# A hybrid decoder block on one core: the last four chunks of w_out split during attention and loaded into h's places by pairs of k, output blocks handed out with 17 steps left

## The chip, the cores and the metric

The kernel runs on one core of one Trainium2 chip. The metric is the device time of one execution in microseconds (us); for the kernel before it is the median of three runs. Engines are named as in the profile: PE does matrix products, PEld loads their weights, DVE is the vector engine, ACT the scalar engine, POOL the general one, and SP issues the DMAs.

## What is computed

One decoder block over 1024 tokens of width 1024, in float32: a token mixer, then a squared-ReLU MLP, each with a norm before and after, a modulation from a conditioning vector and a gate.

```python
mod = cond @ w_ada + b_ada                     # six vectors: sh_a, sc_a, gt_a, sh_m, sc_m, gt_m
h = rms_norm(x, g_attn_pre) * (1 + sc_a) + sh_a
proj = h @ w_in                                # qa, ka, va, qb, kb, vb; rotary on part of q and k
oa = banded_attention(qa, ka, va, 127, sink=sink_a)    # mixer A: 8 query heads on 2 kv heads
ob = dilated_mixture_attention(qb, kb, vb)             # mixer B: 8 heads, three dilated windows
mixed = concat([rms_norm(oa, g_mix_a), rms_norm(ob, g_mix_b)])
y = mixed @ w_out
x = x + gt_a * rms_norm(y, g_attn_post)
h = rms_norm(x, g_mlp_pre) * (1 + sc_m) + sh_m
x = x + gt_m * rms_norm(square(relu(h @ w_up)) @ w_down, g_mlp_post)
```

## The kernel before

**Numbers in two parts.** For accuracy every operand of a large product is split into a part that the fast matmul format holds and the rest: a = hi + lo. Each product is three matmuls (hi hi, hi lo, lo hi) of 128 rows by 512 columns. One engine makes hi (a cast, mostly on ACT) and another lo (a subtraction, on DVE or POOL). The weights w_in, w_out, w_up and w_down and the activations all go through this.

**Stages.** At first the modulation and the norm of x are worked out and h, transposed and modulated, is written to the buffer `hw` by `mod_chunk` (L677). `hw` has 8 places of two parts (hi and lo) of 128 partitions by 1024 numbers. Before the change place t holds the 128 tokens of block t for all 8 chunks of k (128 each), so a matmul over 512 tokens (`proj_mm`, L858) reads four places with a stride.

Then come the projections in 6 units u (two of mixer A, one for each kv head, then four of mixer B, two heads each), each of two halves x of the tokens and three tiles c (q, k, v); `proj_tile` (L917) issues the 8 steps over k of one tile, three matmuls a step. `st.d` counts units done (0 to 6). Attention runs beside them: `items` lists pieces of attention (unit, query block, head), 48 in all, each a chain: scores `s_ps` on PE (L1127, L1182), maximum and masking on DVE (`mn`, L1146, L1197), exponentials on ACT (L1153, L1202), scaling on POOL (`p_sb`, L1158, L1214), a transposition on PE (`pt_ps`, L1232, L1239), the split of the result into `ph` by ACT (L1246) and DVE (L1250), and the product with v on PE (`o_ps`, L1262, L1274). ACT and DVE take it out of PSUM to `ot` and a DMA stores it to the scratch tensor `o_dram` (L1301, L1319). `st.att` counts finished items.

The weights of the modulation are loaded in the background too, into the stage slots, and summed up by POOL (`ada_acc`, L1015). A stage slot is one of five buffers of 128 by 1024 numbers (`r_stg`); the rope products of each unit (DVE L762 to L765, then ACT L768 and POOL L771) take them as well.

**The output stage.** `load_wo` (L1339) becomes due when at most two projection tiles are left to hand out. For each of 8 chunks k it loads 128 rows of w_out raw into a stage slot (L1348), and makes hi on ACT (L1353) and lo on DVE (L1356) or on POOL (L1361, L1362), whichever the planner takes, into place k of `hw`. A place of h can only be overwritten when the last projection tile of its half has read it: `r_wo` counts the places that are free, four given by the last step of each of the two tiles of unit 5, c = 2 (L931). `open_out` (L1367) comes when all are split and the projections are done: it closes the pools of the projections, loads the gate (`gate_a`, L1377) and lets `feed_out` (L1399) hand out the 8 output blocks, one of 128 tokens after another, when their items are finished and at most 10 dense steps are left in PE's queue. `out_block` (L1417) loads `o_sb` from `o_dram` (L1423), casts it to `oh` (L1436) and `ol`, takes the sum of squares by a matmul (`pm_o`, L1452), issues 16 steps of y (L1478 to L1480, three matmuls a step), and works out the post-norm, the gate, the residual, the norm before the MLP (`xn`, L1532) and its transposition (`px`, L1541), which gives the MLP's input. Then the MLP's products (`mlp_ps`, L1912 to L1914) fill PE.

**The order.** At build time a planner (`Sched`) plays the work on five engines with cost formulas. An operation is ready by its dependencies (`deps`) and by counted resources (`takes` and `gives`). Each engine takes the ready step with the earliest start, then the lower `prio`; a step that has two engines to choose from goes to the one that ends it first. PE has streams (`dense` for projections, y and the MLP, `s` and `t` for attention, `misc`, `xt`), with a preference among them that depends on how far the projections are ahead of attention (`prefer`, L2064). Functions in `sc.launch` are called again and again until they hand out their work. What comes out is a fixed order for each engine: on the chip every engine, and the DMA queue of SP too, goes through its list in order and waits at each instruction for the semaphores it needs. So one moved operation changes the order of many.

Of the kernel before, what the change touches and what calls it, by code (L numbers as in the profile page):

```python
# [10 lines left out]
F32 = mybir.dt.float32  # L11
F32R = mybir.dt.float32r
# [3 lines left out]
ALU = mybir.AluOpType  # L16
# [3 lines left out]
P = 128  # L20
D = 1024
S = 1024
KC = D // P
TB = S // P
# [150 lines left out]
class Sched:  # L175
# [20 lines left out]
    def op(self, eng, dur, emit, deps=(), **kw):  # L196

        o = self.step(dur, emit, deps, **kw)
        o.alts = None
        if isinstance(eng, str):  # L200
            self.queue[eng].append(o)
        else:
            o.alts = dict(zip(eng, zip(dur, emit)))
            for e in eng:
                self.queue[e].append(o)
        return o.ev
# [113 lines left out]
def t_sb(n):  # L320
    return 0.098 + 0.00083 * n
# [6 lines left out]
def t_dv(n):  # L328
    return 0.066 + 0.00104 * n
# [6 lines left out]
def t_ptt(n):  # L336
    return 0.19 + 0.0021 * n


def t_pts(n):  # L340
    return 0.28 + 0.00083 * n
# [7 lines left out]
def hybrid_block(ctx: ExitStack, tc: tile.TileContext, x, positions, w_ada, b_ada, g_attn_post, w_in, w_out,  # L349
# [94 lines left out]
    def stage(name):  # L444
        if st.stgp is None:
            return ring_r(name)
        return st.stgp.tile([P, 1024], F32, name=name, tag="stg")

    def load(emit, nbytes, deps=(), takes=(), prio=5, gives=(), after=None, n=1):
        return op("SP", nbytes / (345e3 if prio > -500 else 370e3), emit, deps, takes=takes, prio=prio, gives=gives, after=after, n=n)  # L450
# [226 lines left out]
    def mod_chunk(k, eg, half):  # L677
        t0, t1 = (0, TB) if half is None else (4 * half, 4 * half + 4)
        n = (t1 - t0) * P
        ks = slice(k * P, (k + 1) * P)  # L680
        h, hh = xnT[:, k, t0 * P:t1 * P].rearrange("p (b t) -> p b t", t=P), hw[:, t0:t1, 0, ks]
        deps = [eg] + (e_xn[0] + e_xn[1] if half is None else e_xn[half])

        def full(eng):
            if eng is A:
                return lambda: A.activation(h, h, AF.Identity, bias=s_a[:, k:k + 1], scale=g_a[:, k:k + 1])
            return lambda: V.tensor_scalar(h, h, g_a[:, k:k + 1], s_a[:, k:k + 1], ALU.mult, ALU.add)

        eh = op("ACT", t_sb(n) + 2 * AP_COST, lambda: A.activation(hh, h, AF.Identity, bias=s_a[:, k:k + 1],
                                                                  scale=g_a[:, k:k + 1]), deps, prio=0)  # L690
        e = op("ACT", t_sb(n) + 2 * AP_COST, full(A), [eh], prio=0)
        e = op("DVE", t_dv(n), lambda: V.tensor_tensor(hw[:, t0:t1, 1, ks], h, hh.bitcast(F32), ALU.subtract), [e],
               prio=0)
        for x in (0, 1) if half is None else (half,):
            e_hh[k, x], e_hl[k, x] = eh, e
# [162 lines left out]

    def proj_mm(ps, u, c, k, x, part):
        i, n = w_at(u, c, k)  # L860
        t, w = slice(k * P, (k + 1) * P), w_hl[u, i]
        n = slice(n * P, n * P + P)
        h = [hw[:, 4 * x:4 * x + 4, i, t] for i in range(2)]
        ps = ps[:].rearrange("p (b t) -> p b t", t=P)
        if part != 1:
            T.matmul(ps, w[:, 0, n], h[0], start=(k == 0), stop=False)  # L866
            T.matmul(ps, w[:, 1, n], h[0], start=False, stop=False)  # L867
        if part != 0:
            T.matmul(ps, w[:, 0, n], h[1], start=False, stop=(k == KC - 1))  # L869
# [50 lines left out]
    def proj_tile(u, x, c):  # L920
        b = []
        for k in range(KC):
            def emit(k=k):
                if k == 0:
                    b.append(pj.tile([P, 512], F32, name="pj", tag="pj"))
                proj_mm(b[0], u, c, k, x, None)
            gives = []
            if x and k % 4 == 3:
                gives.append((r_w, 1))
            if u == 5 and c == 2 and k == KC - 1:  # L930
                gives.append((r_wo, 4))  # L931
            d = dense(0.681, emit, [w_e[u, w_at(u, c, k)[0]]], takes=[(r_pj, 1)] if k == 0 else [], gives=gives, after=tick)
        evac(u, x, c, lambda: b[0], d, r_pj)

# [401 lines left out]
    NSTG2 = 4  # L1336
    ph2 = Tok()

    def load_wo():  # L1339

        if len(todo_dense) > 2 or ada.i < NADA:
            return False
        ph2.e_wo, ph2.raw = {}, {}
        eh = None
        for k in range(KC):
            def f_l(k=k):
                ph2.raw[k] = stage("wo_st")
                nc.sync.dma_start(ph2.raw[k][:], w_out[k * P:(k + 1) * P])  # L1348
            e = load(f_l, 524288, takes=[(r_stg, 1), (r_wo, 1)], prio=-8)
            g = cols[:, 56 + k:57 + k]  # L1350

            def f_h(k=k, g=g):
                A.mul(hw[:, k, 0], ph2.raw[k][:], g)  # L1353

            def f_lo(k=k, g=g):
                V.scalar_tensor_tensor(hw[:, k, 1], ph2.raw[k][:], g, hw[:, k, 0].bitcast(F32), ALU.mult,  # L1356
                                       ALU.subtract)
            eh = op("ACT", t_sb(D) + AP_COST, f_h, [e] + ([eh] if eh else []), prio=4)

            def f_lo2(k=k, g=g):  # L1360
                G.tensor_scalar(ph2.raw[k][:], ph2.raw[k][:], g, 1.0, ALU.mult, ALU.mult)  # L1361
                G.tensor_tensor(hw[:, k, 1], ph2.raw[k][:], hw[:, k, 0].bitcast(F32), ALU.subtract)  # L1362
            ph2.e_wo[k] = op(("DVE", "POOL"), (t_dv(D) + AP_DV, t_pts(D) + t_ptt(D)), (f_lo, f_lo2), [eh],
                             gives=[(r_stg, 1)], prio=4)
        return True

    def open_out():  # L1367
# [30 lines left out]

    def feed_out():  # L1399
        tb = ph2.tb  # L1400
        if tb < TB and st.att >= 42 + 2 * (tb // 2) and len(sc.pe.get("dense", [])) <= 10:
            out_block(tb)
            ph2.tb += 1
        return ph2.tb == TB
# [308 lines left out]
    def sums(h, p):  # L1713

        t = half(h)
        fr = t.free
        up_ = h % 2 == 0
        own_a = h == 0 or not up_
        if p == "P1":
            fr.update({"T1": joins(r_raw, 2), "T3": joins(r_raw, 1), "B22": joins(r_raw, 3), "T4": joins(r_raw, 1),  # L1720
                       "T2": joins(r_raw, 2)})
            if h == 0:
                t.a = {q: h2[q] for q in h2}
                t.e_a = dict(e_h2)
                t.ring = r_h2
                t.new = ring_r
            elif not up_:
                u = half(h - 1)
                t.a, t.e_a, t.ring = dict(u.c), {}, r_u
                t.new = lambda n: ring_l(n, F32)  # L1730
            if h == 0 or not up_:
                fr.update({"S1": joins(t.ring, 2), "S3": joins(t.ring, 1), "S2": joins(t.ring if h else r_u, 2),
                           "S4": joins(t.ring, 1), "A22": joins(t.ring, 2)})
        if own_a and h:
            for q, e in half(h - 1).e_c.items():
                t.e_a.setdefault(q, e)
        ea, eb = events(h)
        sum_ = partial(add_up, 10 + ml.seq.index((h, p)))
        if p == ("P6" if h else "P5"):
            sum_(t.b, t.e_b, eb, r_raw, None, "T1", "12", "11", ALU.subtract, [], t.sp["B", "11"], "11")  # L1740
            if not h:
                first_sums(t)
        if p == "P6":
            sum_(t.b, t.e_b, eb, r_raw, ring_r, "T2", "22", "T1", ALU.subtract, [fr["B22"], fr["T1"]], None, None)
            if h == 0:
                second_sums(t)
            elif own_a:
                sum_(t.a, t.e_a, ea, t.ring, t.new, "S1", "21", "22", ALU.add, [fr["A22"]], None, None)
                sum_(t.a, t.e_a, ea, t.ring, None, "S3", "11", "21", ALU.subtract, [], [[e] for e in t.e_a["S1"]], "21")
                sum_(t.a, t.e_a, ea, t.ring, None, "S2", "S1", "11", ALU.subtract, [fr["S1"]],  # L1750
                     [x + [t.e_a["S3"][j]] for j, x in enumerate(t.sp["A", "11"])], "11")
        if p == "P7":
            sum_(t.b, t.e_b, eb, r_raw, None, "T3", "22", "12", ALU.subtract, [fr["B22"]], [[e] for e in t.e_b["T1"]],
                 "12")
        if p == "P3" and own_a:
            sum_(t.a, t.e_a, ea, t.ring, None, "S4", "12", "S2", ALU.subtract, [fr["S2"]], t.sp["A", "12"], "12")
        if p == "P4":
            sum_(t.b, t.e_b, eb, r_raw, None, "T4", "21", "T2", ALU.subtract, [fr["T2"]], t.sp["B", "21"], "21")
# [331 lines left out]
```

## Time and profile before

| what | value |
| --- | --- |
| median of three runs | 1146.05 us (1145.21 to 1146.7) |
| the profiled execution | 1144.1 us |
| its span, from the first to the last instruction of the profile | 1142.2 us |
| mean granted TensorE clock | 0.991 of full speed |
| PE busy, share of the span | 97% |
| DMA traffic | 185.29 MB, mean 162 GB/s |
| projections and attention | to about 380 us; attention without projections to about 437 us |
| output stage, then MLP | to about 535 us, then to the end |

The profiled execution is 1.95 us below the median and holds 1.9 us outside its span. A row of a timeline gives start and length in us, engine, line, operation, what it writes and reads, and how many like it follow each other; brackets hold the idle time of the engine before it and what ended it. Matmuls are pipelined: the distance of their starts is what one costs, not its length. L is a line of the kernel before; in the changed kernel the lines behind L1336 stand some 30 lower.

### The profile page before, as it was taken

How to read it: one execution, taken by the hardware profiler on the slowest of the kernel's cores; microseconds unless marked ns; L12 is line 12 of the kernel's file. 1: busy time of each engine (PE TensorE's matmuls, PEld its weight loads, DVE VectorE, ACT ScalarE, POOL GpSimd, SP SyncE). 2: the span in 40 equal slices, each digit the busy share in tenths (PEclk: the TensorE clock that was granted, in tenths of full speed). 3: DMA queues.
4: the chain of work that ended last, by engine and by line, in shares of the span. 5: the costliest groups of instructions: out<-in, count | busy, mean ns of one | idle time of the engine just before them, and what ended most of it. 6: DMA issues, size and time to landing. Idle time of an engine off the chain costs nothing.

```text
span 1142.2 us, 15600 instructions
## 1 busy us (share of the span) xinstructions
PE 1113.5 (97%) x5417; PEld 925.2 (81%) x5417; DVE 819.3 (72%) x1378; ACT 636.1 (56%) x1101; POOL 267.8 (23%) x349
## 2 busy tenths in 40 slices
PE   8999999999999899998999999999999999999996
PEld 7788878888888687887888888888888888888885
DVE  7878666666667766668879664599644896537998
ACT  8868865464556755676675434553244733246542
POOL 2458867565743521112000000000000000000002
PEclk9999999999999899999999999999999999999998
DMA  9565545343423305555780168712469112584103
GB/s 351 187 208 164 164 155 168 136 155 125 141 77 133 127 26 186 185 202 217 284 310 19 56 230 292 280 41 70 152 245 331 55 56 86 202 304 164 37 19 148
DMA packets 90910, 185.29 MB, mean 162 GB/s; under 512 B 8400, under 2 KB 31056, under 8 KB 90832
## 3 DMA queue, kind: packets, MB, share of 16 engines
q1 hardware_dynamic: 90832, 184.30, 46.1%
q8 instruction: 43, 0.70, 0.2%
q14 instruction: 35, 0.29, 0.1%
HBM read 137.08 MB, written 28.31 MB: 145 GB/s over the span
## 4 chain that ended last, share of the span: by engine, by line
PE 77%; DVE 8%; ACT 4%; issue 4%; POOL 3%; DMA 3%; SPq 0%; DVEq 0%; POOLq 0%; ACTq 0%
PE mlp_ps L1913 17%; PE mlp_ps L1914 17%; PE mlp_ps L1912 17%; PE pj L866 4%; PE pj L869 4%; PE pj L867 4%; PE s_ps L1127 3%; PE o_ps L1262 2%; PE y_ps L1478 1%; PE pt_ps L1232 1%; PE y_ps L1479 1%; PE y_ps L1480 1%; PE pt_ps L1235 1%; DMA o_sb<-o_dram 1%; PE o_ps L1267 1%
## 5 line engine op out<-in xcount | busy, mean ns | idle before, releaser
L1912 PE MATMUL mlp_ps<-hw 128*128 128x512 f32 x896 | 349.8, 390 | 0.0
L1913 PE MATMUL mlp_ps<-hw 128*128 128x512 f32 x896 | 348.8, 389 | 0.0
L1914 PE MATMUL mlp_ps<-hw 128*128 128x512 f32 x896 | 348.8, 389 | 0.0
L1912 PEld LDWEIGHTS mlp_ps<-hw 128*128 128x128 f32 x896 | 168.5, 188 | 35.5 <-issue 0.5
L1913 PEld LDWEIGHTS mlp_ps<-hw 128*128 128x128 f32 x896 | 168.4, 188 | 35.2 <-issue 0.5
L1914 PEld LDWEIGHTS mlp_ps<-hw 128*128 128x128 f32 x896 | 168.4, 188 | 34.9
L1676 DVE TENSOR_TENSOR hw<-w,hw 128x1024 fp32r<-128x1024 f32 x96 | 114.7, 1222 | 95.5 <-ACT hw L1669 95.2
L1669 ACT CAST hw<-w 128x1024 fp32r<-128x1024 f32 x96 | 97.7, 1047 | 128.1 <-PE mlp_ps L1914 97.5
L2012 POOL TENSOR_TENSOR st<-st,nhalf 128x1 f32<-128x1 f32 x8 | 7.8, 977 | 598.5 <-DVE st L2010 598.5
L866 PE MATMUL pj<-hw,w_hl 128*128 128x512 f32 x240 | 102.9, 429 | 0.0
L869 PE MATMUL pj<-hw,w_hl 128*128 128x512 f32 x240 | 95.1, 396 | 0.0
L867 PE MATMUL pj<-hw,w_hl 128*128 128x512 f32 x240 | 94.9, 395 | 0.0
L1250 DVE TENSOR_TENSOR ph<-pt_ps,ph 128x512 fp32r<-128x512 f32 (+1 forms) x110 | 69.5, 648 | 32.9 <-ACT ph L1246 32.6
L1669 ACT CAST hw<-u 128x1024 fp32r<-128x1024 f32 x48 | 48.6, 1051 | 64.6 <-PE mlp_ps L1914 64.6
L1246 ACT CAST ph<-pt_ps 128x512 fp32r<-128x512 f32 (+1 forms) x110 | 59.0, 556 | 31.2 <-PE pt_ps L1235 26.1
L1153 ACT ACTIVATE p_sb<-p_sb,mn 128x128 f32<-128x128 f32 (+3 forms) x64 | 49.7, 777 | 38.7 <-DVE mn L1146 37.2
L1676 DVE TENSOR_TENSOR hw<-u,hw 128x1024 fp32r<-128x1024 f32 x48 | 57.1, 1221 | 18.2 <-ACT hw L1669 18.2
L1970 DVE TENSOR_TENSOR yacc<-yacc,mlp_ps 128x512 f32<-128x512 f32 x96 | 62.3, 685 | 3.3 <-PE mlp_ps L1914 3.3
L1158 POOL TENSOR_SCALAR p_sb<-p_sb,den 128x128 f32<-128x128 f32 (+3 forms) x64 | 48.6, 765 | 55.4 <-DVE den L1156 50.8
L1015 POOL TENSOR_TENSOR ada_acc<-ada_acc,wa_st 128x512 f32<-128x512 f32 x42 | 54.9, 1307 | 3.5
L869 PEld LDWEIGHTS pj<-hw,w_hl 128*128 128x128 f32 x240 | 45.4, 189 | 10.6
L1478 PE MATMUL y_ps<-hw,oh 128*128 128x512 f32 x128 | 52.0, 406 | 0.0
(206 smaller groups left out, 2015.8 us busy)
## 6 DMA issues: line engine op xcount, KB each, us to landing
hw<-s_dram SPq DMA_DIRECT2D x84, 512.0 KB, 4.2
wa_st<-in_w_ada SPq DMA_DIRECT2D x32, 512.0 KB, 4.3
w<-in_w_up SPq DMA_DIRECT2D x32, 512.0 KB, 4.9
w<-in_w_down SPq DMA_DIRECT2D x32, 512.0 KB, 7.0
s_dram<-hw SPq DMA_DIRECT2D x28, 512.0 KB, 3.4
qt<-hl SPq DMA_DIRECT2D x40, 256.0 KB, 2.6
w_st<-in_w_in SPq DMA_DIRECT2D x36, 256.0 KB, 2.9
x_sb<-in_x SPq DMA_DIRECT2D x16, 512.0 KB, 6.5
```

The lines of the kernel that those rows point to most:

```text
L866: T.matmul(ps, w[:, 0, n], h[0], start=(k == 0), stop=False)
L867: T.matmul(ps, w[:, 1, n], h[0], start=False, stop=False)
L869: T.matmul(ps, w[:, 0, n], h[1], start=False, stop=(k == KC - 1))
L1246: A.copy(b["ph"][:, 0, :w], b["pt"][:, :w])
L1250: V.tensor_tensor(b["ph"][:, 1, :w], b["pt"][:, :w], b["ph"][:, 0, :w].bitcast(F32), ALU.subtract)
L1478: T.matmul(ps[:], b["oh"][:, k], wh[:, c0:c0 + 512], start=(k == 4 * m), stop=False)
L1669: A.copy(out[j][0], flat(src[j]))
L1676: V.tensor_tensor(out[j][1], flat(src[j]), out[j][0].bitcast(F32), ALU.subtract)
L1912: T.matmul(ps[m][:], sh, mh, start=starts and k == 0, stop=False, **kw)
L1913: T.matmul(ps[m][:], sh, ml_, start=False, stop=False, **kw)
L1914: T.matmul(ps[m][:], sl, mh, start=False, stop=k == 3, **kw)
L1970: e = op("DVE", t_dv(512), lambda: V.tensor_tensor(y(), y(), ps[m][:], ALU.add), [e, ml.e_y[tb, n]], gives=gives, prio=1)
```

## The change

It has three parts.

1. **The layout of h.** Place 4x + j of `hw` now holds the chunks 2j and 2j + 1 of k for the 512 tokens of half x, each contiguous. The matmuls of the projections read 512 contiguous columns of one place. `proj_tile` gives one `r_wo` with each odd step k of the tiles of unit 5, c = 2, instead of four with the last.
2. **Chunks 4 to 7 of w_out.** A new function hands out `split_wo(k)` when `st.d` passes 2.2, 3.0, 3.8 and 4.6: a raw load into a stage slot, hi on ACT into a second slot, lo on DVE over the raw data, and a store of each to scratch tensors (`wo_dram`). `load_wo` keeps chunks 0 to 3 as they were, but for lo, which only DVE makes now, and adds for chunks 4 to 7 two loads each of 512 KB from the scratch tensors straight into the places, one `r_wo` each. It also waits for the four splits to have been handed out.
3. **Hand-out.** `feed_out` hands out an output block when at most 17 dense steps are left instead of 10.

```diff
--- before.py
+++ after.py
@@ -677,8 +677,8 @@
     def mod_chunk(k, eg, half):
         t0, t1 = (0, TB) if half is None else (4 * half, 4 * half + 4)
         n = (t1 - t0) * P
-        ks = slice(k * P, (k + 1) * P)
-        h, hh = xnT[:, k, t0 * P:t1 * P].rearrange("p (b t) -> p b t", t=P), hw[:, t0:t1, 0, ks]
+        h = xnT[:, k, t0 * P:t1 * P].rearrange("p (x t) -> p x t", t=512)
+        hh, hl = (hw[:, t0 // 4 * 4 + k // 2:t1 - 3 + k // 2:4, i, k % 2 * 512:k % 2 * 512 + 512] for i in range(2))
         deps = [eg] + (e_xn[0] + e_xn[1] if half is None else e_xn[half])
 
         def full(eng):
@@ -689,7 +689,7 @@
         eh = op("ACT", t_sb(n) + 2 * AP_COST, lambda: A.activation(hh, h, AF.Identity, bias=s_a[:, k:k + 1],
                                                                   scale=g_a[:, k:k + 1]), deps, prio=0)
         e = op("ACT", t_sb(n) + 2 * AP_COST, full(A), [eh], prio=0)
-        e = op("DVE", t_dv(n), lambda: V.tensor_tensor(hw[:, t0:t1, 1, ks], h, hh.bitcast(F32), ALU.subtract), [e],
+        e = op("DVE", t_dv(n), lambda: V.tensor_tensor(hl, h, hh.bitcast(F32), ALU.subtract), [e],
                prio=0)
         for x in (0, 1) if half is None else (half,):
             e_hh[k, x], e_hl[k, x] = eh, e
@@ -858,10 +858,9 @@
 
     def proj_mm(ps, u, c, k, x, part):
         i, n = w_at(u, c, k)
-        t, w = slice(k * P, (k + 1) * P), w_hl[u, i]
-        n = slice(n * P, n * P + P)
-        h = [hw[:, 4 * x:4 * x + 4, i, t] for i in range(2)]
-        ps = ps[:].rearrange("p (b t) -> p b t", t=P)
+        w, n = w_hl[u, i], slice(n * P, n * P + P)
+        h = [hw[:, 4 * x + k // 2, i, k % 2 * 512:k % 2 * 512 + 512] for i in range(2)]
+        ps = ps[:]
         if part != 1:
             T.matmul(ps, w[:, 0, n], h[0], start=(k == 0), stop=False)
             T.matmul(ps, w[:, 1, n], h[0], start=False, stop=False)
@@ -927,8 +926,8 @@
             gives = []
             if x and k % 4 == 3:
                 gives.append((r_w, 1))
-            if u == 5 and c == 2 and k == KC - 1:
-                gives.append((r_wo, 4))
+            if u == 5 and c == 2 and k % 2:
+                gives.append((r_wo, 1))
             d = dense(0.681, emit, [w_e[u, w_at(u, c, k)[0]]], takes=[(r_pj, 1)] if k == 0 else [], gives=gives, after=tick)
         evac(u, x, c, lambda: b[0], d, r_pj)
 
@@ -1336,13 +1335,46 @@
     NSTG2 = 4
     ph2 = Tok()
 
+    wo_dram = [[dram.tile([P, 1024], F32, name=f"wo_dram{k}_{i}") for i in range(2)] for k in range(4, KC)]
+    e_wod = {}
+
+    def split_wo(k):
+
+        raw, hi = [], []
+        g = cols[:, 56 + k:57 + k]
+
+        def f_l():
+            raw.append(stage("wo_st"))
+            nc.sync.dma_start(raw[0][:], w_out[k * P:(k + 1) * P])
+        e = load(f_l, 524288, takes=[(r_stg, 1)], prio=21)
+
+        def f_h():
+            hi.append(stage("wo_hi"))
+            A.mul(hi[0][:].bitcast(F32R), raw[0][:], g)
+        eh = op("ACT", t_sb(D) + AP_COST, f_h, [e], takes=[(r_stg, 1)], prio=9)
+
+        def f_lo():
+            V.scalar_tensor_tensor(raw[0][:].bitcast(F32R), raw[0][:], g, hi[0][:], ALU.mult, ALU.subtract)
+        el = op("DVE", t_dv(D) + AP_DV, f_lo, [eh], prio=9)
+        e_wod[k] = [load(lambda t=t, i=i: nc.sync.dma_start(wo_dram[k - 4][i][:], t[0][:]), 524288, [e_],
+                         gives=[(r_stg, 1)], prio=22) for i, (t, e_) in enumerate(((hi, eh), (raw, el)))]
+
+    def feed_wo():
+        k = 4 + len(e_wod)
+        if st.d > WO_AT[k - 4]:
+            split_wo(k)
+        return len(e_wod) == 4
+
+    WO_AT = (2.2, 3.0, 3.8, 4.6)
+    sc.launch.append(feed_wo)
+
     def load_wo():
 
-        if len(todo_dense) > 2 or ada.i < NADA:
+        if len(todo_dense) > 2 or ada.i < NADA or len(e_wod) < 4:
             return False
         ph2.e_wo, ph2.raw = {}, {}
         eh = None
-        for k in range(KC):
+        for k in range(4):
             def f_l(k=k):
                 ph2.raw[k] = stage("wo_st")
                 nc.sync.dma_start(ph2.raw[k][:], w_out[k * P:(k + 1) * P])
@@ -1356,12 +1388,12 @@
                 V.scalar_tensor_tensor(hw[:, k, 1], ph2.raw[k][:], g, hw[:, k, 0].bitcast(F32), ALU.mult,
                                        ALU.subtract)
             eh = op("ACT", t_sb(D) + AP_COST, f_h, [e] + ([eh] if eh else []), prio=4)
-
-            def f_lo2(k=k, g=g):
-                G.tensor_scalar(ph2.raw[k][:], ph2.raw[k][:], g, 1.0, ALU.mult, ALU.mult)
-                G.tensor_tensor(hw[:, k, 1], ph2.raw[k][:], hw[:, k, 0].bitcast(F32), ALU.subtract)
-            ph2.e_wo[k] = op(("DVE", "POOL"), (t_dv(D) + AP_DV, t_pts(D) + t_ptt(D)), (f_lo, f_lo2), [eh],
-                             gives=[(r_stg, 1)], prio=4)
+            ph2.e_wo[k] = op("DVE", t_dv(D) + AP_DV, f_lo, [eh], gives=[(r_stg, 1)], prio=4)
+        for k in range(4, KC):
+            def f_d(k=k):
+                for i in range(2):
+                    nc.sync.dma_start(hw[:, k, i].bitcast(F32), wo_dram[k - 4][i][:])
+            ph2.e_wo[k] = load(f_d, 1048576, e_wod[k], takes=[(r_wo, 1)], prio=-8, n=2)
         return True
 
     def open_out():
@@ -1398,7 +1430,7 @@
 
     def feed_out():
         tb = ph2.tb
-        if tb < TB and st.att >= 42 + 2 * (tb // 2) and len(sc.pe.get("dense", [])) <= 10:
+        if tb < TB and st.att >= 42 + 2 * (tb // 2) and len(sc.pe.get("dense", [])) <= 17:
             out_block(tb)
             ph2.tb += 1
         return ph2.tb == TB
@@ -1720,7 +1752,7 @@
             fr.update({"T1": joins(r_raw, 2), "T3": joins(r_raw, 1), "B22": joins(r_raw, 3), "T4": joins(r_raw, 1),
                        "T2": joins(r_raw, 2)})
             if h == 0:
-                t.a = {q: h2[q] for q in h2}
+                t.a = h2
                 t.e_a = dict(e_h2)
                 t.ring = r_h2
                 t.new = ring_r
```

## The prediction

> **What bounds the kernel now.** I read the page's busy shares first, then the windows by stage, then PE's waits, and last the timelines of each engine in the two stretches where PE stands idle and the change is at work. From the page:
>
> ```profile
> PE 1113.5 (97%) x5417; PEld 925.2 (81%) x5417; DVE 819.3 (72%) x1378; ACT 636.1 (56%) x1101; POOL 267.8 (23%) x349
> ```
>
> PE is the bound, so the time moves only where PE idles or runs at a reduced clock. The span is 1142.2 us, so about 29 us of PE's time are idle. The windows tell where (columns: window, length, busy time of PE, PEld, DVE, ACT and POOL, granted clock, DMA share, GB/s):
>
> ```profile
> 136.00:160.00 24.00, 22.20 (x116) 18.37 (x115) 14.90 (x44) 14.02 (x41) 16.64 (x27) 0.93 0.41 125
> 340.00:380.00 40.00, 39.90 (x237) 34.09 (x236) 27.23 (x68) 24.17 (x48) 12.71 (x13) 1.00 0.45 165
> 380.00:400.00 20.00, 15.30 (x79) 12.42 (x78) 16.92 (x44) 17.48 (x34) 13.61 (x12) 0.83 0.24 70
> 437.00:535.00 98.00, 92.70 (x442) 76.02 (x441) 70.43 (x117) 66.86 (x103) 18.38 (x21) 0.98 0.55 194
> 149.60:153.10 3.50, 3.50 (x10) 2.75 (x9) 2.68 (x7) 2.63 (x10) 1.84 (x5) 0.51 0.35 111
> 392.00:398.90 6.90, 6.23 (x24) 5.38 (x25) 4.98 (x18) 4.88 (x10) 5.15 (x6) 0.51 0.57 172
> ```
>
> Three places that the change touches lose time: 1.8 us at 136 to 160, 4.7 us at 380 to 400 (the last attention items and the splits of w_out), 5.3 us in the output stage. The last two rows show that a granted clock of one half follows the first two, for 3.5 and 6.9 us. In 340 to 380, where the projections fill PE, it loses 0.1 us. PE's waits (us in total, times, longest):
>
> ```profile
> PE px L1541 <- ACT xn L1532: 4.4, 2, 2.9
> PE o_ps L1262 <- DVE ph L1250: 3.2, 5, 1.3
> PE s_ps L1182 <- DVE mn L1197: 1.8, 1, 1.8
> PE pt_ps L1232 <- POOL p_sb L1158: 1.2, 2, 0.8
> PE o_ps L1262 <- ACT ph L1246: 0.6, 1, 0.6
> PE pm_o L1452 <- DVE rs_t L1515: 0.4, 1, 0.4
> PE pm_o L1452 <- ACT junk L1506: 0.3, 1, 0.3
> ```
>
> **Part 1: w_out's last chunks at 380 to 400.** PE's timeline (the last line is the last projection), a start, a length, and in brackets the idle time before it and who ended it:
>
> ```profile
> 383.19 0.33 PE L1232 MATMUL pt_ps<-head,p_sb 128*128 128x128 f32 x1 [0.81 <-POOL p_sb L1158]
> 387.13 0.38 PE L1262 MATMUL o_ps<-ph,v_hl 128*128 128x256 f32 x1 [0.81 <-DVE ph L1250]
> 390.56 0.39 PE L1262 MATMUL o_ps<-ph,v_hl 128*128 128x256 f32 x1 [0.56 <-ACT ph L1246]
> 392.27 0.58 PE L1262 MATMUL o_ps<-ph,v_hl 128*128 128x256 f32 x1 [1.32 <-DVE ph L1250]
> 396.45 0.47 PE L1232 MATMUL pt_ps<-head,p_sb 128*128 128x128 f32 x1 [0.40 <-POOL p_sb L1158]
> 397.86 0.78 PE L1478 MATMUL y_ps<-hw,oh 128*128 128x512 f32 x1
> 398.86 0.39 PE L1480 MATMUL y_ps<-hw,ol 128*128 128x512 f32 x1
> 399.77 0.41 PE L1262 MATMUL o_ps<-ph,v_hl 128*128 128x256 f32 x2
> 401.68 0.58 PE L1452 MATMUL pm_o<-ones,o_sb 128*128 128x1 f32 x4
> 376.65 0.40 PE L869 MATMUL pj<-hw,w_hl 128*128 128x512 f32 x1
> ```
>
> What the late engines were doing just then, on ACT, DVE, POOL and the DMA queue (the line of L1356 holds all five DVE splits: ns of the shortest, the median and the longest, and the first and the last start):
>
> ```profile
> 387.31 2.19 ACT L1353 ACTIVATE hw<-wo_st,head 128x1024 fp32r<-128x1024 f32 x2
> 396.32 1.05 ACT L1436 CAST oh<-o_sb 128x1024 fp32r<-128x1024 f32 x1 [0.55 <-DMA o_sb<-o_dram]
> L1356 DVE SCALAR_TENSOR_TENSOR hw<-wo_st,head,hw x5: 1276/1285/2481, 352.6 to 388.8; 128x1024 fp32r<-128x1024 f32 x5
> 391.55 0.67 DVE L1250 TENSOR_TENSOR ph<-pt_ps,ph 128x512 fp32r<-128x512 f32 x1
> 392.36 2.38 POOL L1362 TENSOR_TENSOR hw<-wo_st,hw 128x1024 fp32r<-128x1024 f32 x1
> 391.75 0.38 SPq L1423 DMA_DIRECT2D o_sb<-o_dram  x1
> ```
>
> The splits of chunks 4 to 7 stand in the in-order queues of ACT, DVE and POOL among the softmax's own casts. Two ACT splits (to 389.50) put off the cast that PE needs at 390.56; DVE's last and longest split (388.8 + 2.48 = 391.3) puts off the ph of 391.55, for which PE waits 1.32 us; POOL's last ends at 394.74 and p_sb comes after it. The change takes all of these splits out of this stretch: 0.81 + 0.56 + 1.32 + 0.40 = 3.1 us of waits. The wait of 383.19 stands before them and stays. The slow clock costs 6.23 x (1 - 0.51) = 3.05 us of PE's work. So up to 6.1 us can go.
>
> In their place stand eight loads of 512 KB straight into h's places, which the last projection frees pair by pair, the last pair at its end, 377.0. With the slowest landing of a raw load (6.9 us, the row in part 3) the last of them is there at 384 (an estimate), where the last split of before ended at 394.74. So the weight is no longer late. Next is the first output block itself: its y needs o_sb, which needs the last store of o_dram before it. Before, gate_a and with it o_sb also stood on the queue behind that DVE split (to 391.3, then 391.75). Now the store decides, some 1 to 2 us sooner: y at about 396.0 rather than 397.86. In the changed order the first y_ps also stands ten PE groups later (1341st against 1331st), so that more attention is done by then: eight attention groups ran from 399.77 to 401.68, hence ten are 2.4 us. Together 1.9 + 2.4 = **-4.3 us**. At the bad end only part goes, as items without projections between them stay held by DVE (16.92 of 20 us busy, 5.0 of it w_out): -1.4. At the good end -6.1.
>
> A half clock follows a wait here. [...]
>
> **Part 2: output blocks at 17.** A block's load and oh, ol and squares are queued 7 steps earlier. The waits for pm_o in PE's list (0.4 + 0.3 us) get ahead of time. The first px and the last do not hang on the hand-out alone:
>
> ```profile
> 439.13 1.09 PE L1541 MATMUL px<-head,xn 128*128 128x128 f32 x8 [1.51 <-ACT xn L1532]
> 532.31 1.97 PE L1541 MATMUL px<-head,xn 128*128 128x128 f32 x8 [2.91 <-ACT xn L1532]
> ```
>
> The last has no further block to hide behind and stays; the first may shrink. I take 0.7 + 0.3 = **-1.0**, bounds -2.2 (0.7 + 1.51) and +2.7: in the changed order 42 y matmuls stand among the attention groups instead of 54, and twelve times 0.23 us is the cover that the last items lose.
>
> **Part 3: chunk 4, at 136 to 160.** Here the change takes a slot, a load, an ACT split, a DVE split and two stores:
>
> ```profile
> 148.79 0.74 PE L1182 MATMUL s_ps<-kt,qt 128*128 128x256 f32 x4 [1.80 <-DVE mn L1197]
> 145.02 0.68 DVE L762 TENSOR_TENSOR hl<-pj,tab 64x512 f32<-64x512 f32 x1 [4.90 <-POOL ada_acc L1015]
> 147.94 0.62 ACT L768 CAST hl<-hl 128x512 fp32r<-128x512 f32 x1 [4.37 <-POOL wa_st L1014]
> 148.58 0.58 ACT L1309 COPY otmp<-o_ps 64x512 f32<-64x512 f32 x1
> DMA to landing us min/median/max: 3.9/5.1/6.9
> ```
>
> Before, DVE's rope waits for a stage slot that POOL gives up just before 145.02, and PE loses 1.80 us. In the changed order rope gets an earlier slot and starts some 4 us sooner (its 4.90 us of idle time, less what ACT's tables need); the wo_st load gets the slot of 145.0. So PE's wait goes (-1.8). But wo_hi stands in ACT's queue ahead of the hl cast, of otmp and of the ph casts, and it waits for that load. A raw load lands 3.9 to 6.9 us after its issue (the last row, that of the eight loads of L1348, four and four at a time); a lone one I put at 3.9. ACT is then held to 145.0 + 3.9 + 1.1 (one split, 2.19 / 2) = 150.0 instead of 147.94; the casts and the copy behind it (0.62 + 0.58 + half of the 1.03 in part 5) end at 151.7, so the o_ps that needs ph waits from about 148.9, where PE stood at 148.79 before, to 151.7: +2.8. The half clock (3.5 x 0.49 = 1.7 us) I leave as it is, as a wait of the same sort stands there again. Sum **+1.0**. Bounds: both gone, -1.8 - 1.7 = -3.5; the slowest landing, +2.8 + 3.0 - 1.8 = +4.0.
>
> **Part 4: chunks 5 to 7.** Each adds 1.1 us to ACT (2.19 / 2) and 1.3 to DVE (the median split) at 190 to 295, with the projections between the items; PE's list has no wait there of the kind that these would lengthen, and ACT and DVE are 56% and 72% busy. The eight stores of 512 KB go on SP behind o_dram's. **0**, bounds 0 and +2 if one hangs behind its load as chunk 4 does.
>
> **Part 5: chunks 0 to 3.** In the changed order ACT's first split comes earlier, before the ph cast at 345.47, and waits for the raw load of 341.05; DVE gets the split that POOL had.
>
> ```profile
> 345.47 1.03 ACT L1246 CAST ph<-pt_ps 128x384 fp32r<-128x384 f32 x2 [2.46 <-PE pt_ps L1235]
> 345.99 1.24 DVE L1250 TENSOR_TENSOR ph<-pt_ps,ph 128x384 fp32r<-128x384 f32 x2 [2.13 <-ACT ph L1246]
> 341.05 2.78 SPq L1348 DMA_DIRECT2D wo_st<-in_w_out  x4
> ```
>
> With the first load landing at 345.5 (4.4 us, between its 3.9 and 5.1) and 1.1 us of split, the cast moves from 345.47 to 346.6, and a DVE split of 1.3 can stand before its other half: ph ends 1.9 us later than at 347.2. PE has projections to fill part of that. **+1.0**, bounds 0 and +2.2.
>
> **Part 6: the layout of h.** The same number of matmuls with contiguous instead of strided columns; y_ps and the projections already start 0.23 us apart (398.86 to 399.77 holds four). **0.**
>
> **Sum.** -4.3 - 1.0 + 1.0 + 0 + 1.0 + 0 = -3.3 us. The profiled execution took 1144.1 us (its span and 1.9 around it), 1.95 below the median of the runs; the change is taken off both: 1140.8 profiled, 1142.7 as median.
>
> **Rivals.**
> (a) *The wait only moves.* Attention without projections is held by DVE, the o_sb chain gives no earlier y, and the clock halves again at 392 as there are waits left: part 1 gives -1.4, the rest (-1.0 + 1.0 + 1.0) +1.0: -0.4, so 1145.6. For it speaks DVE's 16.92 of 20 us; against it the 5.0 us of w_out in those.
> (b) *The head of ACT's queue.* wo_hi waits for its load at chunk 4 as long as the slowest landing (+4.0) and at another chunk (+2), the early split of chunk 0 costs its bound (+2.2), while part 1 gives its poor half (about -3) and part 2 its -1.0: +4.2, so 1150.3. It decides from a landing of about 5.5 us after issue on. For it speaks that ACT goes in order and nothing stands between; against it that 512 KB at 136 to 160 have a DMA share of 0.41 beside them. This one is slower.
> (c) *Both stalls end.* The chunk 4 load lands within ACT's idle 4.37 us, so 1.80 and its half clock go (-3.5) and part 1 gives -5; with -1.0 and +1.0: -8.5, so 1137.5.
>
> **Chances.** A change of 0.2% (2.3 us) is about what a measurement can tell from none. Forecast (1139.5 to 1143.7, faster) 0.45; (a) 0.21, of which 0.17 within 0.2% and the rest just faster; (b) 0.24 slower; (c) 0.10 faster. The range takes in (c)'s near side, (a) and most of (b): 1138.0 to 1149.5; above 1149.5 and below 1138.0 I leave about 0.1 each. Faster 0.45 + 0.10 + 0.04 = 0.59, same 0.17, slower 0.24.
>
> **What the changed profile would show.** Part 1: no split in 380 to 400, the wo_dram loads landed before 386, y_ps first at about 396 after ten more attention groups, and a granted clock in that window above 0.83. Part 2: no pm_o in PE's waits; the px wait of 2.9 us still there. Part 3: s_ps L1182's wait gone and one of an o_ps near 150 in its place. Part 5: a short PE wait near 348. It is wrong if PE still idles over 4 us at 380 to 400, or if any wait over 2 us stands behind an ACT split.

## The result, and the profile after

The changed kernel's median is 1142.74 us (1140.55 to 1145.95, 19 runs), beside 1144.88 us (1143.13 to 1147.45, 19 runs) of the kernel before, of which more runs were made. The ratio is 0.998, 95% interval 0.9972 to 0.9988: faster by 2.1 us. Forecast were 3.3 us less and 1142.7. That the second number is met so closely is luck: it started from 1146.05, the median of three runs of the kernel before, which came out 1.2 us lower with 19. The profiled execution of the changed kernel has a span of 1141.0 us.

The windows by stage of the changed kernel (the columns are those of the prediction):

```profile
136.00:160.00 24.00, 21.13 (x115) 16.91 (x115) 14.04 (x38) 14.73 (x40) 18.41 (x28) 1.00 0.48 138
160.00:340.00 180.00, 177.06 (x1001) 149.49 (x1001) 122.10 (x316) 102.38 (x224) 116.39 (x128) 1.00 0.50 168
340.00:380.00 40.00, 37.94 (x223) 32.39 (x222) 27.31 (x66) 22.11 (x44) 9.67 (x11) 1.00 0.39 135
380.00:400.00 20.00, 17.61 (x115) 14.61 (x114) 15.38 (x48) 15.47 (x35) 5.93 (x8) 1.00 0.76 273
437.00:535.00 98.00, 92.92 (x445) 75.69 (x444) 72.85 (x130) 58.48 (x85) 16.16 (x19) 1.00 0.52 185
```

Of the kernel before, the one of these rows that the prediction did not need:

```profile
160.00:340.00 180.00, 179.15 (x1015) 151.62 (x1014) 118.97 (x309) 100.00 (x220) 115.29 (x125) 1.00 0.41 136
```

Subtract PE's busy time from the length: PE's idle time at 380 to 400 fell from 4.70 to 2.39 us, POOL's busy time there from 13.6 to 5.9, and the clock is 1.00 instead of 0.83. But 136 to 160 went from 1.80 to 2.87 us of idle time, 160 to 340 from 0.85 to 2.94, and 340 to 380 from 0.10 to 2.06. The change won behind the projections and lost beside them. These are single executions, and the row from 160 to 340 cannot carry much: other kernels of the experiments have the same order there, and lose 2.25 us with the order of before (out17_only) and 1.35 us with that of the changed kernel (hand_out_10):

```profile
160.00:340.00 180.00, 178.65 (x1011) 150.96 (x1009) 123.01 (x316) 103.32 (x225) 116.73 (x129) 1.00 0.50 168
```

At 136 to 160 both orders repeat: 1.78 and 2.87 us. The rows of the last line of the projections and of the first line of the MLP put a number on gain and loss (first and last start, us). Before:

```profile
L869 PE MATMUL pj<-hw,w_hl x240: 387/393/632, 68.6 to 376.6; 128*128 128x512 f32 x120
L1912 PE MATMUL mlp_ps<-hw x896: 387/389/792, 514.7 to 1131.5; 128*128 128x512 f32 x180
```

Changed:

```profile
L868 PE MATMUL pj<-hw,w_hl x240: 387/394/403, 69.4 to 381.8; 128*128 128x512 f32 x120
L1944 PE MATMUL mlp_ps<-hw x896: 387/389/792, 513.7 to 1130.1; 128*128 128x512 f32 x180
```

| stretch | before | changed | difference |
| --- | --- | --- | --- |
| this line's first to last projection | 308.0 | 312.4 | +4.4 |
| from there to the MLP's first matmul | 138.1 | 131.9 | -6.2 |
| both | 446.1 | 444.3 | -1.8 |

The second difference is firm: the four profiles of kernels that split all of w_out late have 137.1 to 139.2 us there, the ten others 131.8 to 133.5. The first depends on the execution: hand_out_10, with the same order of the projections as the changed kernel, has 309.9, a loss of 1.9.

PE's waits in the changed kernel:

```profile
PE px L1573 <- ACT xn L1564: 3.2, 1, 3.2
PE o_ps L1273 <- ACT ph L1245: 2.5, 1, 2.5
PE pv L836 <- ACT vt L830: 2.5, 3, 2.1
PE o_ps L1261 <- DVE ph L1249: 1.9, 5, 0.6
PE pm_o L1484 <- DVE o_sb L1478: 1.7, 4, 0.5
...
PE o_ps L1273 <- DVE ph L1249: 1.2, 2, 1.0
...
PE pt_ps L1231 <- POOL p_sb L1157: 0.8, 1, 0.8
```

The wait of s_ps for the rope (1.8 us) is gone, o_ps of L1261 (L1262 before) waits for DVE's ph 1.9 us in all where it waited 3.2, and px waits once instead of twice. The second line is new, and the third was one wait of 0.3 us before: both of their long waits, 2.5 and 2.1 us, stand behind a w_out split on ACT. The first of them, on PE, ACT, DVE and the DMA queue:

```profile
149.50 0.40 PE L868 MATMUL pj<-hw,w_hl 128*128 128x512 f32 x1
152.43 0.51 PE L1273 MATMUL o_ps<-ph,v_hl 128*128 128x512 f32 x1 [2.53 <-ACT ph L1245]
```

```profile
143.96 0.67 ACT L723 ACTIVATE tab<-ptab,head 128x512 f32<-128x512 f32 x1
149.51 1.15 ACT L1353 ACTIVATE wo_hi<-wo_st,head 128x1024 fp32r<-128x1024 f32 x1 [4.88 <-DMA wo_st<-in_w_out]
150.56 0.60 ACT L768 CAST hl<-hl 128x512 fp32r<-128x512 f32 x1
151.19 0.58 ACT L1308 COPY otmp<-o_ps 64x512 f32<-64x512 f32 x1
151.79 1.07 ACT L1245 CAST ph<-pt_ps 128x512 fp32r<-128x512 f32 x2
```

```profile
142.12 0.69 DVE L762 TENSOR_TENSOR hl<-pj,tab 64x512 f32<-64x512 f32 x1 [0.95 <-ACT tab L723]
```

```profile
146.07 0.35 SPq L1348 DMA_DIRECT2D wo_st<-in_w_out  x1
```

DVE's rope starts 2.9 us sooner than before, as it no longer waits for POOL's slot. The raw load of chunk 4 is issued at 146.07 and lands 3.4 us later, and ACT, which had nothing left at 144.6, stands 4.88 us in front of the split; the cast that PE needs comes third behind it.

### The profile page after: what moved, and what is told of

The parts are those of the page before. It is cut to its first block, busy times and chain, and to the rows that moved or that the text cites. A ratio compares the mean times of both kernels' runs of the same rounds, so it can differ in the third digit from the quotient of the medians.

```text
span 1141.0 us, 15625 instructions
## 1 busy us (share of the span) xinstructions
PE 1108.6 (97%) x5417; PEld 919.1 (81%) x5417; DVE 823.8 (72%) x1396; ACT 629.3 (55%) x1083; POOL 258.5 (23%) x346
## 4 chain that ended last, share of the span: by engine, by line
PE 77%; DVE 9%; ACT 4%; DMA 4%; issue 3%; POOL 2%; SPq 0%; DVEq 0%; POOLq 0%; ACTq 0%
PE mlp_ps L1945 17%; PE mlp_ps L1946 17%; PE mlp_ps L1944 17%; PE pj L865 4%; PE pj L866 4%; PE pj L868 4%; PE s_ps L1126 3%; PE o_ps L1261 2%; PE y_ps L1510 2%; PE y_ps L1512 1%; PE y_ps L1511 1%; DMA wo_st<-in_w_out 1%; PE pt_ps L1231 1%; DVE h L1592 1%; PE s_ps L1181 1%
```

## The experiments

Twelve kernels, each timed against the kernel before on the same chip. Theory 1: the late splits of w_out cost what the prediction said, and the change gives part of it back where ACT stands at the head of its queue in front of a load. Its first rival: the gain is the layout's or the hand-out's. Its second: the losses are the clock's doing.

| run | median us | ratio to before, 95% interval |
| --- | --- | --- |
| the change as a whole | 1142.74 | 0.9980 (0.9972 to 0.9988) |
| layout_only | 1145.24 | 1.0001 (0.9992 to 1.0010) |
| out17_only | 1144.91 | 1.0002 (0.9990 to 1.0015) |
| no_early_split | 1148.88 | 1.0037 (1.0023 to 1.0051) |
| hand_out_10 | 1141.67 | 0.9976 (0.9966 to 0.9987) |
| late_0_to_3 | 1142.17 | 0.9983 (0.9972 to 0.9994) |
| late_5_to_7 | 1140.87 | 0.9967 (0.9954 to 0.9979) |
| chunk_4_at_2_6 | 1140.53 | 0.9969 (0.9958 to 0.9979) |
| late_chunk_4 | 1137.30 | 0.9933 (0.9919 to 0.9946) |
| late_4_to_7 | 1135.03 | 0.9920 (0.9904 to 0.9935) |
| late_4_to_7_out10 | 1135.30 | 0.9918 (0.9905 to 0.9932) |
| late_all | 1136.15 | 0.9926 (0.9913 to 0.9939) |
| late_all_out10 | 1133.71 | 0.9906 (0.9893 to 0.9918) |

### The parts alone

**layout_only**: the kernel before with `mod_chunk`, `proj_mm` and `proj_tile` of the changed one, and the last line of its diff. **out17_only**: the kernel before with

```diff
-        if tb < TB and st.att >= 42 + 2 * (tb // 2) and len(sc.pe.get("dense", [])) <= 10:
+        if tb < TB and st.att >= 42 + 2 * (tb // 2) and len(sc.pe.get("dense", [])) <= 17:
-                t.a = {q: h2[q] for q in h2}
+                t.a = h2
```

> The kernel before with the first part of the change alone: h's layout by pairs of k, and places freed by pairs. Theory 1 (a contiguous column read costs what a strided one costs; the pairs let raw loads of w_out start some steps earlier, which alone brings nothing as the splits end late anyway): ratio to before 1.000 within 0.001. Rival (the loss of no_early_split, ratio 1.0037, is the layout's, because the earlier loads put the splits among other work): ratio 1.003 to 1.005, with PE's waits for ph or ot at 350 to 390 us longer than before.

> The kernel before with the third part of the change alone: output blocks handed out at 17 steps left. Theory 1: pm_o's waits change by a microsecond at most and y's place among attention a little: ratio to before 0.999 to 1.001. Rival (the loss of no_early_split, ratio 1.0037, is the earlier hand-out's): ratio 1.003 to 1.005, with the loss after 380 us.

Measured 1.0001 and 1.0002: neither does anything alone, as theory 1 says, and the first rival falls for each.

**no_early_split**: the changed kernel with `load_wo` of before and without `split_wo`; **hand_out_10**: the changed kernel with 10 in place of 17.

> The changed kernel with its second part undone: h's layout by pairs and the hand-out at 17 stay, but all eight chunks of w_out are loaded raw and split at the end, as in the kernel before (POOL may take a lo part again). Theory 1 (the weights' splits were late, and part of what the early split gains is lost again where ACT stands behind a load): PE's idle time at 380 to 400 us comes back from 2.4 to 4.5 us or more, the waits of 2.5 us near 150 and of 2.1 us near 351 go, and the 1.8 us at the rope near 146 comes back; ratio to before 0.9985 to 1.0005. Rival (the gain came from the layout and the hand-out): ratio 0.998, as with the whole change.

> The changed kernel with the hand-out of output blocks at 10 steps left, as before. Theory 1: the hand-out moves waits of pm_o and nothing else, so the ratio to before stays at 0.998 within 0.0008, and pm_o's waits, 1.7 us in the changed kernel, fall to about 0.7 us. Rival (the earlier hand-out is part of the gain, about 1 us as I had put it): ratio 0.999.

Without the early split the gain is gone, and more: 1.0037, above the 1.0005 that I gave it. With the same layout and hand-out, the early split is thus worth 6.5 us (1.0037 less 0.9980). Its windows and a wait:

```profile
380.00:400.00 20.00, 15.88 (x79) 13.28 (x78) 16.25 (x43) 13.56 (x29) 9.65 (x8) 0.74 0.37 124
```

```profile
PE pv L836 <- DVE ot L1297: 4.1, 2, 2.5
```

4.12 us are idle again at 380 to 400, somewhat less than the 4.5 that I expected, and the clock is lower than before, 0.74. The 2.5 us wait is one for `ot`, which stands on DVE behind a lo split of 2.21 us. The layout alone has a like wait (2.4 us) and loses nothing by it in the median, so why layout and hand-out lose 4 us together and nothing each stays open. What the profiles show of it is the clock: a mean of 0.74 in this stretch, beside 0.91 in layout_only's and 0.83 in out17_only's, one execution each. hand_out_10 is where theory 1 put it, 0.9976: the hand-out at 17 adds nothing to the change.

### The head of ACT's queue

In these kernels the planner is told that a raw load lands later than its formula says; nothing else is edited. The order that comes out has ACT's split further back.

```diff
+    def late_load(emit, d, **kw):
+        box = []
+
+        def after():
+            box[0].t += d
+        box.append(load(emit, 524288, after=after, **kw))
+        return box[0]
...
-        e = load(f_l, 524288, takes=[(r_stg, 1)], prio=21)
+        e = late_load(f_l, 5.0, takes=[(r_stg, 1)], prio=21)
```

This is late_4_to_7; late_chunk_4 has `5.0 if k == 4 else 0.0`, late_5_to_7 `0.0 if k == 4 else 5.0`, and late_0_to_3 has 3.0 in `load_wo` in its place.

> The changed kernel, but the planner is told that the raw loads of chunks 4 to 7 land 5 us later than its formula says, so that ACT's split stands further back in its queue; nothing else is edited. Theory 1 (ACT stands at the head of its queue waiting for the load, and PE's o_ps waits 2.5 us for the ph behind it): that wait goes, and the ones of 0.6 and 0.7 us near 214 and 252 at most shrink; 2 to 3 us faster than the changed kernel, ratio to before 0.9955 to 0.9965. Rival (those waits are covered later, or the difference between the kernels is only the clock): ratio 0.998.

> As late_4_to_7, but only chunk 4's load is told to land 5 us later. Theory 1 (chunk 4 is the one whose split stands at ACT's head while its load is under way): nearly all of late_4_to_7's gain over the changed kernel, that is the 2.5 us wait of o_ps, the ones that follow it to 160 us (about 1.5 us) and the half clock after them (1.7 us): 5 to 6.5 us faster than the changed kernel, ratio to before 0.9925 to 0.994. Rival (all four chunks cost alike): a quarter of the gain, ratio 0.9963.

> As late_4_to_7, but only the loads of chunks 5 to 7 are told to land 5 us later; chunk 4 stays as changed. Theory 1: the waits for ph at 214 and 252 us (0.6 to 1.3 us together) go, the 2.5 us wait near 150 stays: 1 to 2 us faster than the changed kernel, ratio to before 0.9963 to 0.9972. Rival (all four chunks cost alike): three quarters of the gain, ratio 0.9935.

late_4_to_7 gains more than twice what I had put on it: 9.2 us less than before, and by the ratios (0.9980 less 0.9920) 6.9 less than the changed kernel, where I expected 2 to 3. I had counted the wait and not what came after it. late_chunk_4, expected after that, holds 5.4 of it (0.9980 less 0.9933, in the range that theory 1 gave), late_5_to_7 1.5 (0.9967, likewise). The rival of equal shares falls. ACT in late_chunk_4:

```profile
143.97 0.67 ACT L723 ACTIVATE tab<-ptab,head 128x512 f32<-128x512 f32 x1
145.06 0.62 ACT L768 CAST hl<-hl 128x512 fp32r<-128x512 f32 x1 [0.41 <-ACT tab L723]
147.27 0.58 ACT L1308 COPY otmp<-o_ps 64x512 f32<-64x512 f32 x1 [1.59 <-PE o_ps L1273]
147.88 1.08 ACT L1245 CAST ph<-pt_ps 128x512 fp32r<-128x512 f32 x2
...
150.33 1.14 ACT L1361 ACTIVATE wo_hi<-wo_st,head 128x1024 fp32r<-128x1024 f32 x1
```

The load is issued at the same time as in the changed kernel (146.06), but the casts run 3.9 to 5.5 us sooner, before it lands, and the split then starts without a wait. Its window, and the one of late_4_to_7 behind it:

```profile
136.00:160.00 24.00, 23.88 (x133) 19.92 (x134) 19.25 (x58) 18.65 (x55) 20.97 (x32) 1.00 0.58 181
```

```profile
160.00:340.00 180.00, 179.64 (x1026) 153.19 (x1025) 120.90 (x305) 101.27 (x214) 116.58 (x125) 1.00 0.50 169
```

PE's idle time fell from 2.87 to 0.12 us in the first, and from 2.94 to 0.36 in the second, where the order of the changed kernel lost 1.35 us in hand_out_10. The same chunks are split in the same stretch, on the same engines and with the same DMAs, so the early split's work costs PE next to nothing there. The planner moves more than the split (the rope's lo part goes from POOL to DVE, at 150.10), but up to the 2.5 us wait of the changed kernel the orders of PE and DVE are the same and ACT's is not: that wait is shown to be the doing of the place in ACT's queue. For the rest of the 5.4 us it is argued.

**chunk_4_at_2_6** tells the slot from the queue:

```diff
-    WO_AT = (2.2, 3.0, 3.8, 4.6)
+    WO_AT = (2.6, 3.0, 3.8, 4.6)
```

> The changed kernel with one number edited: chunk 4 is split when 2.6 units of projections are done instead of 2.2, in the next unit's attention, where ACT's split stands behind a w_in split and before an exponential. In this order DVE's rope near 145 waits for POOL's ada_acc again, as in the kernel before. Theory 1 (two things happened at 2.2: rope got a free stage slot, worth 1.8 us of PE's wait and the half clock after it, and ACT's split stood before its load, 2.5 us and its followers): the 2.5 us wait near 150 goes, the 1.8 us wait near 147 comes back, so about 2 us faster than the changed kernel and 3 slower than late_chunk_4: ratio to before 0.995 to 0.997. Rival (all of late_chunk_4's gain is ACT's queue): ratio 0.9925 to 0.994.

Measured 0.9969, in theory 1's range and outside the rival's. The wait of before is back:

```profile
PE s_ps L1181 <- DVE mn L1196: 1.7, 1, 1.7
```

So late_chunk_4 is 3 to 4 us faster than this one (1140.5 less 1137.3 by the medians, 0.9969 less 0.9933 by the ratios). What differs between them at 136 to 160 is the slot that rope gets when chunk 4 is split at 2.2, and by the profiles' idle time (1.75 and 0.12 us) it is worth 1.6 us. The queue takes part again: at chunk 4's new place ACT stands in front of its load too, and three waits of PE for the ph behind it follow, 1.64 us, where late_chunk_4 has none up to 200 us:

```profile
171.08 1.16 ACT L1353 ACTIVATE wo_hi<-wo_st,head 128x1024 fp32r<-128x1024 f32 x1 [2.20 <-DMA wo_st<-in_w_out]
173.28 0.50 PE L1273 MATMUL o_ps<-ph,v_hl 128*128 128x512 f32 x1 [0.46 <-ACT ph L1245]
174.35 0.50 PE L1273 MATMUL o_ps<-ph,v_hl 128*128 128x512 f32 x1 [0.57 <-DVE ph L1249]
179.81 0.50 PE L1273 MATMUL o_ps<-ph,v_hl 128*128 128x512 f32 x1 [0.61 <-DVE ph L1249]
```

The two profiled executions are no measure of the sum: their spans, 1137.5 and 1137.1 us, differ by 0.4, as the first is faster and the second slower than its kernel's median.

**late_0_to_3** was to take away the second new wait.

> The changed kernel, but the planner is told that the raw loads of chunks 0 to 3 land 3 us later than its formula says; ACT's first split then stands behind the ph casts and the copy of vt. Theory 1: the wait of pv for vt, 2.1 us near 351, goes; 1.5 to 2.2 us faster than the changed kernel, ratio to before 0.996 to 0.9967, unless the splits now end late for the output stage, which would show as PE's idle time at 380 to 400 above 2.4 us. Rival (projections cover that wait anyway): ratio 0.998.

A miss: 0.9983, no gain that can be told, though its profile has PE busy for all 40 us from 340 to 380. The answer is in hand_out_10, whose order up to 380 is that of the changed kernel:

```profile
340.00:380.00 40.00, 39.94 (x236) 34.20 (x235) 27.18 (x67) 22.83 (x45) 9.30 (x11) 1.00 0.44 157
```

```profile
348.49 1.15 ACT L1385 ACTIVATE hw<-wo_st,head 128x1024 fp32r<-128x1024 f32 x1 [2.25 <-DMA wo_st<-in_w_out]
```

The changed kernel's row was:

```profile
350.87 1.15 ACT L1385 ACTIVATE hw<-wo_st,head 128x1024 fp32r<-128x1024 f32 x1 [4.25 <-DMA wo_st<-in_w_out]
```

ACT stands in front of the load in both, 2.25 us in one execution and 4.25 in the other, and only the longer one reaches PE. The 2.1 us wait of vt is one that some executions have.

### The versions that beat both

> late_4_to_7 with the hand-out at 10 instead of 17. Theory 1 (the hand-out moves small waits of pm_o and px and no more): the ratio to before stays at 0.992 within 0.001. Rival (with the splits out of the way, the early hand-out is what keeps PE filled after 380 us): 0.9935 or more.

> late_4_to_7 with the loads of chunks 0 to 3 told to land 3 us later as well, and the hand-out at 10. Theory 1: the wait of pv for vt near 343 (0.8 us there, 0 to 2.1 us in the other profiles) goes for good, with nothing late behind it: ratio to before 0.991 to 0.992. Rival (as in late_0_to_3, which gained nothing that could be told, the later splits give it back in the last attention items): 0.992 to 0.993, with more idle time at 370 to 395 us than late_4_to_7's.

> The same with the hand-out at 17 as changed. Theory 1: within 0.001 of late_all_out10. Rival (hand-out and later splits of chunks 0 to 3 collide in the last attention items): 0.002 slower than it.

The first is where theory 1 put it. late_all_out10 is the fastest of all, 0.9906 (0.9893 to 0.9918), just below theory 1's range, and vt's wait is gone; but its interval overlaps with that of late_4_to_7_out10, so that step isn't clear of noise. late_all is 0.002 slower, which is the rival's number and not theory 1's, with intervals that overlap. The rival put that into the last attention items; there the two profiles are alike. Some 0.9 of the 2.1 us between the profiles' spans (1131.9 and 1134.0) lie before 340 us, where late_all has a wait of 0.9 us for ot at 191. Three others have it too (1.0 to 1.6 us), out17_only among them, while before, with the same order there, has none: it goes with the execution. The rest lies in the output stage, 3.5 us of idle time at 437 to 535 with the hand-out at 10 and 5.0 at 17. So in none of the five pairs that differ by it did the hand-out at 17 gain, and in this one it may cost 1 to 2 us. What is left of waits over 1 us after the start of late_all_out10 is px's:

```profile
PE px L1581 <- ACT xn L1572: 3.8, 2, 2.9
```

## Why the prediction was right, and where its steps were off

**Part 1 (-4.3) and 2 (-1.0)**: together -6.2 from the last projection to the MLP, against -5.3. The mechanism of part 1 was right: no split stands at 380 to 400, and the eight loads land by

```profile
379.64 3.16 SPq L1395 DMA_DIRECT2D hw<-wo_dram  x4
DMA to landing us min/median/max: 3.8/6.2/7.2
```

379.64 + 3.16 + 7.2 = 390 at the latest, 11 us ahead of y (the estimate, 384, was too early as the projections ended 5 us later; they move 365 GB/s meanwhile). The first y comes at 401.0, 19.2 us after the last projection, where before it was 21.2: -2.0, as the 1.9 of the working, and no wait stands directly before it. By PE's idle time and clock the stretch gave 2.3 us (4.70 less 2.39) and the 3.05 us of the half clock (the prediction's estimate), together 5.4: more than half of that is the clock, which the working had as its good end. The wait for POOL's p_sb that was to stay did stay, 0.81 us. Part 2 was wrong. px's first wait went, but pm_o waits 1.7 us in place of 0.7, four times for the sum of the squares on DVE (L1478); the output stage's idle time went from 5.30 to 5.08 us only, and 3.50 with the hand-out at 10.

**Part 3 (+1.0)**: the forecast of what happens was right to the instruction: s_ps's wait gone, a 2.5 us wait of o_ps near 152 behind hl, otmp and ph. The size was off: of the chain, the followers up to 161 us (two more waits for DVE's ph, 1.2 us, the sixth line of the waits) were not counted, and the price of ACT's order was 5.4 us by late_chunk_4, of which the working had 2.8, and 1.7 of half clock that it left as before.

**Part 4 (0)**: failed. By late_5_to_7 the place of chunks 5 to 7 costs 1.5 us, and by late_chunk_4 and late_4_to_7 as much again (0.9933 less 0.9920), each time with intervals that overlap. The step that failed is "PE's list has no wait there of the kind that these would lengthen": its line of o_ps waiting for DVE's ph has five waits, two of which stand at 213 and 246 us, 0.3 us each. They stayed, with one of 0.4 us for ACT's ph in front of the first; another of 0.6 us came beside chunk 6's split (not in hand_out_10's execution) and one of 0.2 us beside chunk 7's, and late_5_to_7 has but one of 0.3 us left between 160 and 320.

**Part 5 (+1.0)**: between 0 and 2.1 us, by the execution; in the median not to be told. **Part 6 (0)**: right, 1.0001.

Rival (b) had the right place and the right mechanism; its point of decision, a landing 5.5 us after issue, was not reached: chunk 4's came 3.4 us after it. Rival (c)'s gain, 8.5 us, is close to what late_chunk_4 measures when the queue is put right: 7.6 (1144.91 less 1137.30). By the text's own test ("any wait over 2 us stands behind an ACT split") the forecast's reasoning was in trouble, as two such waits are there: the total came out near because, in the profiled pair, a gain 0.9 us larger than forecast (6.2, not 5.3) stood against losses 2.4 us larger (4.4, not 2.0). That they balanced so is luck.

**The clock.** I left its half stretches as they were in part 3 and took 3.05 us of them as an upper end in part 1. In the profiled execution of the changed kernel there is none before the last 8 us, though PE waits 2.5, 2.1 and 3.2 us:

```profile
149.00:153.00 4.00, 1.41 (x5) 0.56 (x3) 1.20 (x2) 3.45 (x6) 4.00 (x6) 1.00 0.39 158
527.00:536.00 9.00, 5.82 (x31) 4.60 (x30) 6.75 (x11) 5.86 (x11) 3.99 (x1) 1.00 0.34 111
```

hand_out_10 has the same 2.5 us wait, and after it

```profile
153.00:158.00 5.00, 4.78 (x15) 3.26 (x15) 3.45 (x8) 3.34 (x11) 1.77 (x5) 0.66 0.61 148
```

So at this place the second rival explains the scatter of executions: the wait in late_chunk_4 is gone together with what follows it, whichever way the clock falls. At 380 to 400 the clock does go with the kernel: 0.74 to 0.91 in the four profiles of kernels that split all of w_out late, 1.00 in those of the changed kernel, hand_out_10, late_0_to_3, late_4_to_7, late_5_to_7, late_chunk_4, late_all and late_all_out10. This is out17_only, with the 0.83 of before:

```profile
380.00:400.00 20.00, 15.32 (x78) 12.30 (x77) 16.62 (x43) 17.51 (x33) 13.73 (x12) 0.83 0.33 96
```

## What to carry to other kernels

Work that is moved into idle time of an engine must be ready when its turn comes: on an engine that goes in order, a cheap operation that waits for a load holds up everything behind it (ACT's split of 1.15 us stood 4.88 us in front of its load, and the casts behind it ran 3.9 to 5.5 us later than in late_chunk_4), so put the load well ahead of it, or the operation behind the urgent ones; here the move gave 2 us, and 9 with the operation put right. Count what follows a new wait, too, and look at more than one execution before you chase a wait of 2 us. And where two edits each do nothing, measure them together before you keep both.

## What the runs showed of the hardware

A wait of 1.8 to 3.2 us of PE is followed by half clock in some executions and not in others, at the same place. After the 1.8 us of s_ps the clock at 136 to 160 was 0.93 in the kernel before, and 1.00 in layout_only, out17_only and no_early_split; after the 2.5 us of o_ps 0.93 in hand_out_10, late_0_to_3 and late_5_to_7, and 1.00 in the changed kernel. With a wait of px of 3.2 us in each, it was 0.97 at 437 to 535 in late_4_to_7, 0.98 in late_chunk_4 and 1.00 in the changed kernel. In the kernel before the stretches at half clock were 3.41 us long from 149.67, 6.83 from 392.02 and 3.41 from 531.96. What decides whether one follows is not shown. In the 19 runs of the changed kernel the time goes with the mean clock: the six with 0.996 or more have a mean of 1141.7 us, the seven at 0.993 or less 1143.7 us, that is some 2 us for two or three stretches (an estimate: 3.41 us at half clock, as in the kernel before, take 0.0015 off the mean clock).

A lo split on DVE of 128 by 1024 numbers took 1.28 us (the median of five before), but 2.48 us beside POOL's subtraction of the same size before (388.8 and 387.82 us), and 2.21 us in no_early_split at 385.02 us; in the changed kernel, where POOL makes no lo part of w_out, all eight took 1.27 to 1.48 us. That POOL is the reason was not tried.
